# The second FFN product of a two-layer hybrid encoder, from slices of tokens to a 2x2x2 block scheme with seven products

## The chip, the cores and the metric

One core of a Trainium2 chip. TensorE (PE) multiplies a 128x128 block of weights by a tile of up to 512 columns and adds up in PSUM; VectorE (DVE), ScalarE (ACT) and GpSimd (POOL) work on tiles in SBUF (the first two on PSUM as well); SyncE (SP) issues most of the DMAs, GpSimd's queue a few. Each engine runs its own list of instructions in order, and the engines wait for each other by semaphores. The metric is the device time of one run in microseconds (us), lower is better. A profiled execution gives a trace; its span is the time from its first to its last instruction.

## What is computed

A two-layer encoder over 1024 prompt frames and 64 sample frames, 1088 tokens together: a state-space mixer, then attention, each followed by a gated feed-forward network (FFN). The change is in the FFN of both layers:

```python
D_MODEL = 1024; FFN_HIDDEN = 2816          # 22 tiles of 128
def rmsnorm(x, w):
    y = x * rsqrt(mean(x * x, axis=-1) + EPS)
    return y * w
def swiglu(u, w_in, w_out):
    g, up = split(u @ w_in, 2, axis=-1)
    return (silu(g) * up) @ w_out          # w_out: the second FFN product
# for each layer:
x = x + rmsnorm(mixer_or_attention(rmsnorm(x, nw[0])), nw[1])
x = x + rmsnorm(swiglu(rmsnorm(x, nw[2]), ffn_w_in, ffn_w_out), nw[3])
```

## The kernel before

Activations stand as columns: a tile has 128 features on the partitions and tokens along the free axis. Each float32 operand is split into a rounded high part and a low part, and each 128x128 block takes three matmuls: high weight by high input, high by low, low by high. So the work of a product is (row tiles) x (inner tiles) x 3 matmuls for each run of columns.

**The first FFN product** (1024 to 2 x 2816) already uses a 2x2x2 block scheme. The tokens are two blocks b of 512 and 576 columns (`BO`, `BN`), each of two quarters (`QS`: 256, 256, 288, 288 columns). `PRODS` lists seven products P1 to P7 of sums of blocks; `run_pair` computes them for one pair of hidden tiles (gate and value) for both b, adds them up while evicting from PSUM, and stores the hidden tile to DRAM. The first six hidden tiles of block 0 are computed plainly (`plain_pairs`). The sixteen pairs after them are done for both blocks, then six for block 1 alone.

**The second FFN product** (2816 to 1024) is plain. In `back`, the loop over `SL` takes three slices of 384, 384 and 320 tokens; for each slice it goes over eight row tiles m, and for each over three weight chunks of 8, 8 and 6 inner tiles (`KCH`). A task `loader` fetches the hidden tiles of a slice from DRAM into a staging tile `sg` and splits them into the `RX` and `R` tiles; the next slice is loaded while PE is at this one. When a slice is done, the task `end` normalizes it, adds the residual, writes it out, and in layer 0 also prepares the input of the next layer, all beside the next slice's matmuls.

**Weights.** The class `Weights` works through a list (`plan`) in order: `load` brings a chunk from DRAM into a raw tile (two of its own, and one or two lent from `RX`), `part` splits it into one of three `hl` tiles. The usual split is a ScalarE cast (the high part) and a VectorE subtraction (the low part). With `acc` set, ScalarE casts, ScalarE writes the negated high part to the low part's place, and a DMA on GpSimd's queue adds the weight to it from DRAM. Before, `acc` is set for a few chunks of the first FFN product and of the mixer only. A cast into an `hl` tile waits for the last matmul on the chunk that was there, three chunks earlier.

**What sets the order.** The matmuls' order is as the program is written (PE is scheduled by hand); `Stream` lets side tasks run ahead by a planned clock and the waits in their `yield`s (`EP_W`, `ER_W`, `EQ_W`). The other engines' order is made by a scheduler from priorities.

Of the kernel before, what the change touches and what calls it, by code (L numbers as in the profile page):

```python
# [8 lines left out]
F32 = mybir.dt.float32  # L9
# [39 lines left out]
ES = 0.5, 0.5, 0.0  # L49
OS = 1.9, 1.4  # L50
EP_W, ER_W, EQ_W = (9.4, 9.4, 2.2), (8.9, 8.9, 3.3), (11.0, 11.0)
# [4 lines left out]
LDP, ENP, ATP = 1500, (0, 0, 1500), 1000  # L56
# [3 lines left out]
RAWB, HLB, SGB = 2, 3, 5  # L60
# [6 lines left out]
NACC = 3  # L67

# [310 lines left out]
def hybrid_kernel(  # L379
# [42 lines left out]
    hd_ = [dr.tile([P, FT, T], F32, name=f"hscr{i}") for i in range(2)]  # L422
# [834 lines left out]

    def ffn_plan(layer):
        w1, w2 = w_f1[layer], w_f2[layer]
        W.plan(*[dict(src=[w1[i]], acc=t_ < NACC or t_ == NB0 - 1) for t_ in range(NB0) for i in (t_, FT + t_)])  # L1260
        for t_ in [*range(NB0, FT), *range(NB0)]:
            W.plan(dict(src=[w1[t_], w1[FT + t_]], pacc=t_ in (NB0, NB0 + 1)))
# [7 lines left out]
    def plain_pairs(ts, ops, hd, px, tmp):  # L1270

        n = ops.n
        first = ts == PGS[0]
        xs, ws = {}, {}
        for t_, i, q in [(t_, i, q) for t_ in ts for i, q in (((0, 0), (1, 0), (0, 1), (1, 1)) if first else ((0, 0), (0, 1), (1, 0), (1, 1)))]:
# [4 lines left out]
            if i == 0:  # L1280
                xs[t_, q] = tmp.tile([P, n], F32, tag=("p1", "u3")[q] + f"{t_ % 2}", name="x")
# [6 lines left out]
            def mult(ps):  # L1288
                with tc.high_priority(HIP):
                    V.tensor_tensor(x, ps[:, :n], x, op=ALU.mult)  # L1290
                nc.sync.dma_start(hd[:, t_, q * n:(q + 1) * n], x)
# [5 lines left out]
    def run_pair(t_, pr, bs, ends, ops, hd, px, tmp, apart=False):  # L1297
# [3 lines left out]
        for (p_, key, c0, i), b in [(x, b) for b in bs for x in PRODS] if apart else [(x, b) for x in PRODS for b in bs]:  # L1301
# [3 lines left out]
            def t_new(tag):  # L1305
                return tmp.tile([P, n], F32, tag=f"{tag}{b if len(bs) > 1 else t_ % 2}", name=tag)
# [15 lines left out]
            with tc.high_priority(HIP):  # L1322
# [16 lines left out]
                elif p_ == P4:  # L1339
# [3 lines left out]
                    nc.sync.dma_start(hd[:, t_, BO[b] + n:BO[b] + 2 * n], x["u3"])  # L1343
                else:
                    V.tensor_tensor(x["u2"], ps, x["u2"], op=ALU.add)
                    G.tensor_tensor(x["c22"], x["p1"], x["u2"], op=ALU.mult)
                    nc.sync.dma_start(hd[:, t_, BO[b]:BO[b] + n], x["c22"])
# [6 lines left out]
    def back(layer, start, cpost, xsrc, xmid, cpre, cpost2, xout, rb_out, done2):  # L1354

        hd = hd_[layer]
        dn, ops, phase, hid = [], [Ops(0, layer), Ops(1, layer)], [0], [{}, {}, {}]
        with ExitStack() as es:
# [3 lines left out]
            stage[0] = lambda: sgp.tile([P, 384], F32, tag="sg", bufs=SGB, name="sg")  # L1362

            def loader():

                for s, (o, n) in enumerate(SL):
                    yield 0, 0, lambda: phase[0] > (s > 0)
# [693 lines left out]
```

## Time and profile before

| | |
|---|---|
| time, median of three runs | 2938.9 us (2938.18 to 2941.24) |
| span of the profiled execution (no other time of it is given) | 2929.9 us |
| first FFN product, pairs for both blocks and for block 1, layer 0 | to 1315.6 us |
| second FFN product, layer 0 / layer 1, first matmul | 1315.6 / 2653.8 us |
| second FFN product, layer 1, last matmul | 2916.6 us |
| DMA traffic | 369 MB, mean 126 GB/s |

A row of the page's groups gives line, engine, operation, what is written and read, how often, and after the bar the total and mean time of one. Consecutive matmuls overlap, so the distance between two starts tells what one costs. A row of the stretches gives the stretch, then for PE, weight loads, DVE, ACT and POOL the busy time and in brackets the count, then the granted TensorE clock (1.00 is full speed), the share of the DMA engines' time, and GB/s. In a timeline a row has start, duration, engine, line, operation, and in square brackets how long the engine was idle before it and what ended that.

### The profile page before, as it was taken

How to read it: one execution, taken by the hardware profiler on the slowest of the kernel's cores; microseconds unless marked ns; L12 is line 12 of the kernel's file. 1: busy time of each engine (PE TensorE's matmuls, PEld its weight loads, DVE VectorE, ACT ScalarE, POOL GpSimd, SP SyncE). 2: the span in 40 equal slices, each digit the busy share in tenths (PEclk: the TensorE clock that was granted, in tenths of full speed). 3: DMA queues.
4: the chain of work that ended last, by engine and by line, in shares of the span. 5: the costliest groups of instructions: out<-in, count | busy, mean ns of one | idle time of the engine just before them, and what ended most of it. 6: DMA issues, size and time to landing. Idle time of an engine off the chain costs nothing.

```text
span 2929.9 us, 56271 instructions
## 1 busy us (share of the span) xinstructions
PE 2897.3 (99%) x21562; PEld 2858.7 (98%) x21562; DVE 2027.6 (69%) x4452; ACT 1403.6 (48%) x2535; POOL 718.9 (25%) x884
## 2 busy tenths in 40 slices
PE   8999999999999999999999999999999999999999
PEld 8999999999999999999999899999999999999998
DVE  7988878885867555583567887778688554575544
ACT  6655546454544222353445665556664222244443
POOL 1333333331022434350111000000131434351111
PEclk9999999999999999999999999999999999999999
DMA  4423333335564222345664322223476222245654
GB/s 138 133 92 106 104 98 109 100 117 165 165 187 137 76 81 77 108 151 163 207 192 154 98 74 72 65 69 108 132 204 179 83 77 81 75 154 178 225 171 135
DMA packets 203422, 369.12 MB, mean 126 GB/s; under 512 B 20752, under 2 KB 149488, under 8 KB 203152
## 3 DMA queue, kind: packets, MB, share of 16 engines
q1 hardware_dynamic: 199920, 354.97, 38.3%
q0 software_dynamic: 3232, 10.56, 2.0%
q8 instruction: 169, 2.77, 0.4%
q14 instruction: 101, 0.83, 0.1%
HBM read 298.24 MB, written 62.74 MB: 123 GB/s over the span
## 4 chain that ended last, share of the span: by engine, by line
PE 88%; DVE 6%; DMA 2%; ACT 2%; issue 1%; SPq 0%; POOL 0%; DVEq 0%; ACTq 0%; POOLq 0%
PE px L1314 9%; PE px L1315 9%; PE px L1313 9%; PE mm L467 8%; PE mm L469 8%; PE mm L468 8%; PE po L1515 6%; PE po L1516 6%; PE po L1514 6%; PE mmx L468 3%; PE mmx L469 3%; PE mmx L467 3%; PE ptp L1747 2%; PE po L1782 2%; PE S L1716 1%
## 5 line engine op out<-in xcount | busy, mean ns | idle before, releaser
L467 PE MATMUL mm<-r,hl 128*128 128x384 f32 (+2 forms) x1704 | 566.6, 333 | 2.6 <-DVE vt L1679 1.0
L469 PE MATMUL mm<-r,hl 128*128 128x384 f32 (+2 forms) x1704 | 549.6, 323 | 1.0 <-DVE hl L343 0.7
L468 PE MATMUL mm<-r,hl 128*128 128x384 f32 (+2 forms) x1704 | 549.3, 322 | 0.0
L343 DVE TENSOR_TENSOR hl<-raw,hl 128x1024 fp32r<-128x1024 f32 x216 | 256.3, 1187 | 216.6 <-ACT hl L342 208.9
L1314 PE MATMUL px<-r,hl 128*128 128x288 f32 (+1 forms) x1184 | 347.6, 294 | 0.0
L467 PEld LDWEIGHTS mm<-r,hl 128*128 128x128 f32 x1704 | 321.9, 189 | 4.9 <-DVE vt L1679 1.3
L469 PEld LDWEIGHTS mm<-r,hl 128*128 128x128 f32 x1704 | 321.1, 188 | 1.9 <-DVE hl L343 1.0
L468 PEld LDWEIGHTS mm<-r,hl 128*128 128x128 f32 x1704 | 322.2, 189 | 0.3
L1315 PE MATMUL px<-r,hl 128*128 128x288 f32 x1056 | 311.5, 295 | 0.0
L1313 PE MATMUL px<-r,hl 128*128 128x288 f32 x1056 | 310.4, 294 | 0.0
L342 ACT CAST hl<-raw 128x1024 fp32r<-128x1024 f32 x216 | 216.8, 1004 | 162.5 <-PE po L1516 101.6
L493 POOL TENSOR_TENSOR ssum<-ssum,sq 128x256 f32<-128x256 f32 (+3 forms) x97 | 125.5, 1295 | 616.9 <-ACT sq L492 601.3
L1314 PEld LDWEIGHTS px<-r,hl 128*128 128x128 f32 x1184 | 222.4, 188 | 0.0
L1315 PE MATMUL px<-rx,hl 128*128 128x256 f32 x768 | 214.2, 279 | 3.6 <-DVE hl L343 3.5
L1313 PE MATMUL px<-rx,hl 128*128 128x256 f32 x768 | 213.9, 278 | 0.4 <-DVE x L1290 0.4
L1515 PE MATMUL po<-rx,hl 128*128 128x384 f32 (+1 forms) x624 | 202.0, 324 | 0.2
L1313 PEld LDWEIGHTS px<-r,hl 128*128 128x128 f32 x1056 | 198.9, 188 | 0.1
L1315 PEld LDWEIGHTS px<-r,hl 128*128 128x128 f32 x1056 | 198.9, 188 | 0.0
L1514 PE MATMUL po<-rx,hl 128*128 128x384 f32 (+1 forms) x608 | 197.7, 325 | 0.0
L1516 PE MATMUL po<-rx,hl 128*128 128x384 f32 (+1 forms) x608 | 196.7, 324 | 0.0
L1314 PE MATMUL px<-rx,hl 128*128 128x256 f32 x640 | 178.4, 279 | 0.0
L1514 PE MATMUL po<-r,hl 128*128 128x384 f32 (+1 forms) x448 | 148.4, 331 | 0.0
(367 smaller groups left out, 7890.1 us busy)
## 6 DMA issues: line engine op xcount, KB each, us to landing
raw<-in_w_f_dram SPq DMA_DIRECT2D x154, 512.0 KB, 3.7
rx<-in_w_f_dram SPq DMA_DIRECT2D x54, 512.0 KB, 3.7
raw<-in_w_in_dram SPq DMA_DIRECT2D x40, 512.0 KB, 3.7
MT<-ascr SPq DMA_DIRECT2D x48, 384.0 KB, 4.3
sg<-hscr SPq DMA_DIRECT2D x88, 192.0 KB, 3.4
raw<-in_w_f_dram SPq DMA_DIRECT2D x44, 384.0 KB, 3.2
raw<-in_w_so_dram SPq DMA_DIRECT2D x32, 512.0 KB, 3.7
raw<-in_w_o_dram SPq DMA_DIRECT2D x19, 512.0 KB, 3.6
```

What stands on the lines that cost most here:

```text
L342: self.nc.scalar.copy(h, v)
L343: (eng or self.eng or self.nc.vector).tensor_tensor(lo, v, h, op=ALU.subtract)
L467: PE.matmul(ps[:, :n], h_, xh, start=(first and i == 0), stop=False)
L468: PE.matmul(ps[:, :n], h_, xl, start=False, stop=False)
L469: PE.matmul(ps[:, :n], l_, xh, start=False, stop=(last and i == nk - 1))
L493: (eng or G).tensor_tensor(ssum[:, :n], ssum[:, :n], q[:, :n], op=ALU.add)
L1313: PE.matmul(ps, wh, ah[:, k, :], start=(k == 0), stop=False)
L1314: PE.matmul(ps, wh, al[:, k, :], start=False, stop=False)
L1315: PE.matmul(ps, wl, ah[:, k, :], start=False, stop=(k == 3))
L1514: PE.matmul(ps[:, :n], wh, xh, start=(k == 0), stop=False)
L1515: PE.matmul(ps[:, :n], wh, xl, start=False, stop=False)
L1516: PE.matmul(ps[:, :n], wl, xh, start=False, stop=(k == FT - 1))
```

## The change

The second FFN product becomes a 2x2x2 block scheme as well: output rows in two halves of four tiles, inner tiles in two halves of eleven (`KH`), and each b's tokens in two quarters. The seven products are the outermost loop (`SEQ`): P1, P6, P2 and P5 for both b, then P3, P7, P4 for b 0, then the same for b 1, whose weights are fetched and split again. A weight chunk is now six or five inner tiles (768 or 640 columns), and where both b share it, it is held until the second has used it.
- The sums of hidden tiles that the products need are made in SBUF by `hidden`, on VectorE, when a tile is finished, and all seven operands go to DRAM (`hc`). The hidden tiles are computed in another order (`T_PLAIN`, `T_BOTH`, `T_TAIL`), so that the two tiles of a sum are neighbours.
- The sums of weights are made by a side task `w2_sums` beside the first product: four loads, four VectorE operations and four stores for each of sixteen pieces a layer. P1, P2 and P3 read `w_f2` itself and have `acc` set; P4 to P7 read the sums.
- `evict` adds each product to its output blocks (one copy, seven additions on VectorE); the output is held by quarters, and `end` runs by quarter, four times a layer.
- `loader` reads several hidden tiles with one DMA, straight into the low part's tile, without a staging tile.
- In layer 1, `evv` waits until the norms of its slice are there.

```diff
-KCH = ((0, 8), (8, 8), (16, 6))
+    W2S = {P6: 0, P7: 1, P5: 2, P4: 3}
+    SEQ = ((P1, (0, 1)), (P6, (0, 1)), (P2, (0, 1)), (P5, (0, 1)), (P3, (0,)), (P7, (0,)), (P4, (0,)), (P3, (1,)), (P7, (1,)), (P4, (1,)))
+    KCH = (0, 6), (6, 5)
...
-        for s in range(NSL):
-            for m in range(KD):
+        for p_, _ in SEQ:
+            for j in range(4):
                 for k0, nk in KCH:
-                    W.plan(dict(src=[w2[m][:, k0 * P:(k0 + nk) * P]], n=nk * P))
+                    W.plan(dict(src=[w2_of(layer, p_, j)[:, k0 * P:(k0 + nk) * P]], n=nk * P, acc=p_ in (P1, P2, P3)))
...
+    def w2_sums(layer, yet):
+        w2, wd = w_f2[layer], wd_[layer]
+        for j in range(4):
+            for c in range(0, KH * P, SUM_C):
...
+                for t_, m, a in ((b22, j + 4, KH * P + c), (b12, j + 4, c), (b11, j, c), (b21, j, KH * P + c)):
+                    nc.sync.dma_start(t_, w2[m][:, a:a + SUM_C])
+                V.tensor_tensor(b22, b22, b12, op=ALU.subtract)
+                V.tensor_tensor(b12, b12, b11, op=ALU.subtract)
+                V.tensor_tensor(b11, b22, b11, op=ALU.add)
+                V.tensor_tensor(b21, b21, b11, op=ALU.subtract)
+                for i, t_ in enumerate((b11, b22, b12, b21)):
+                    nc.sync.dma_start(wd[:, i, j, c:c + SUM_C], t_)
+                yield 0, SUM_GAP
...
+            def hidden(t_, b, x, z, late=None):
+                if not kh:
+                    s3 = stage[0]()[:, :n] if late is None else late[:, k * n:(k + 1) * n]
+                    out(OPI["a11"], x)
+                    out(OPI["s3"], total(s3, x, z, ALU.subtract))
...
+                out(OPI["a12"], x)
+                out(OPI["a22"], z)
+                out(OPI["s1"], total(z0, z0, z, ALU.add))
+                s2 = total(stage[0]()[:, :n], z, s3, ALU.subtract)
+                out(OPI["s2"], s2)
+                out(OPI["s4"], total(stage[0]()[:, :n], x, s2, ALU.subtract))
...
+            for x, (p_, bs) in enumerate(SEQ):
+                if x == len(SEQ) - 1:
+                    W.lent.cap = 0
+                    st.spawn(end_load(3))
+                for j in range(4):
+                    ws = []
+                    for b in bs:
+                        n = ops[b].n
+                        ps = px.tile([P, 512], F32, tag="mm", name="po")
+                        for c, (k0, nk) in enumerate(KCH):
+                            if b == bs[0]:
+                                ws.append(W.get())
+                            h, v = ws[c]["w"]
+                            for k in range(k0, k0 + nk):
...
+                                PE.matmul(ps[:, :n], wh, xh, start=(k == 0), stop=False)
+                                PE.matmul(ps[:, :n], wh, xl, start=False, stop=False)
+                                PE.matmul(ps[:, :n], wl, xh, start=False, stop=(k == KH - 1))
+                            if b == bs[-1]:
+                                W.put()
+                        evict(p_, b, j, ps[:, :n])
```

Two places of the built programs show what this does to the order. The first is TensorE at the start of a weight chunk in the second FFN product of layer 0 (`po` is the PSUM tile, `rx` the input, `hl` the weights; the number is that of the buffer's use). Before:

```order
L1514 MATMUL po_16083<-rx_15063,hl_16021 128x384 [waits Activation_49]
L1515 MATMUL po_16083<-rx_15063,hl_16021 128x384
L1516 MATMUL po_16083<-rx_15063,hl_16021 128x384 [waits DVE_49]
L1514 MATMUL po_16083<-rx_15068,hl_16021 128x384
L1515 MATMUL po_16083<-rx_15068,hl_16021 128x384
```

TensorE at the start of the second weight chunk of product P2, layer 0, after the change:

```order
L1675 MATMUL po_17085<-rx_16517,hl_16966 128x256
L1676 MATMUL po_17085<-rx_16518,hl_16966 128x256
L1677 MATMUL po_17085<-rx_16517,hl_16966 128x256
L1675 MATMUL po_17085<-rx_16635,hl_16966 128x256
L1676 MATMUL po_17085<-rx_16636,hl_16966 128x256
L1677 MATMUL po_17085<-rx_16635,hl_16966 128x256
L1675 MATMUL po_17085<-rx_16635,hl_17047 128x256 [waits Activation_49]
L1676 MATMUL po_17085<-rx_16636,hl_17047 128x256
L1677 MATMUL po_17085<-rx_16635,hl_17047 128x256 [waits DMASW7_49]
L1675 MATMUL po_17085<-rx_16635,hl_17047 128x256
```

The third matmul of a chunk, the first with the low part of the weight, waited for VectorE and now waits for a DMA of GpSimd's queue (`DMASW`). The second place is ScalarE beside these matmuls. Before:

```order
L342 CAST hl_16050<-raw_15857 128x1024 [waits DVE_49,PE_49,Activation_49]
L1376 CAST r_15972<-sg_15978 128x384 [waits DMAHW0_49]
L1376 CAST r_15977<-sg_15982 128x384 [waits DMAHW1_49]
L1376 CAST r_15986<-sg_15987 128x384 [waits DMAHW2_49]
L1529 COPY y_15939<-po_15940 128x384 [waits DMASW0_49,DMAHW4_49,PE_49,Pool_49]
L342 CAST hl_16073<-rx_15877 128x768 [waits DMAHW3_49,DVE_49,Activation_49]
```

ScalarE in product P2 of layer 0 after the change (`ssum` belongs to the norms):

```order
L343 CAST hl_17078<-rx_16949 128x768 [waits DMAHW1_49,DVE_49,PE_49]
L1446 CAST r_17003<-r_17004 128x1024 [waits DMAHW7_49]
L344 ACTIVATE hl_17078<-hl_17078 128x768 [waits Activation_49]
L1446 CAST r_17017<-r_17018 128x768 [waits DMAHW1_49]
L497 ACTIVATE ssum_17120<-rx_16351 128x256 [waits DVE_49]
L343 CAST hl_17141<-raw_16970 128x640 [waits DMAHW5_49,DMASW6_49,PE_49]
L344 ACTIVATE hl_17141<-hl_17141 128x640 [waits Activation_49]
```

ScalarE has a second operation for each such chunk, and the cast into `hl_17141` waits for TensorE's last use of `hl_16966`, which had the buffer before, and for the DMA that wrote there.

More of the change, by code (lines that the diff above doesn't have):

```diff
@@ L1398, in end @@
-                steps = rb_steps(ss, n, out, ER_W[s], more=more)
+                if more is None:
+                    yield 0, EP_W[q]
+                steps = rb_steps(ss, n, out, ER_W[q], more=more)
                 if more is not None:
```

342 lines of the change are left out of this document (216 added, 126 removed).

## The prediction

> **What bounds the kernel now.** The page comes first: its span and its engines, then the stretches of time around the second FFN product of each layer (both layers, cut at its first and last matmul), then who makes TensorE wait.
>
> ```profile
> span 2929.9 us, 56271 instructions
> PE 2897.3 (99%) x21562; PEld 2858.7 (98%) x21562; DVE 2027.6 (69%) x4452; ACT 1403.6 (48%) x2535; POOL 718.9 (25%) x884
> PE 88%; DVE 6%; DMA 2%; ACT 2%; issue 1%; SPq 0%; POOL 0%; DVEq 0%; ACTq 0%; POOLq 0%
> ```
>
> TensorE (PE) is busy for 99% of the span and is 88% of the chain of waits. The stretches (microseconds, then busy time and count of PE, weight loads, VectorE, ScalarE, GpSimd, then granted clock, DMA share, GB/s) show the same of the two stages that the change touches:
>
> ```profile
> 1020.00:1316.00 296.00, 296.00 (x2355) 296.00 (x2354) 176.54 (x301) 105.06 (x176) 123.47 (x105) 1.00 0.33 104
> 1480.00:1556.00 76.00, 75.79 (x497) 75.14 (x496) 55.33 (x95) 40.20 (x63) 13.99 (x9) 1.00 0.66 211
> 2737.00:2840.00 103.00, 103.00 (x598) 102.94 (x597) 51.78 (x75) 42.41 (x68) 12.03 (x10) 1.00 0.67 216
> PE px L1315 <- DVE hl L343: 3.5, 2, 1.8
> ```
>
> In the first product (1020 to 1316) and in the second (the other two rows) PE never stops; the largest group of PE waits in the whole span is 3.5 us. So columns taken away from PE are time saved, as long as nothing new makes PE wait. That second half of the sentence decides here.
>
> **What the change removes.** A matmul is priced by the distance between starts, not by its listed duration, since matmuls overlap. First and last start of unbroken runs, by the columns that they stream:
>
> ```profile
> 1419.67 0.34 PE L1514 MATMUL po<-r,hl 128*128 128x384 f32 x1
> 1425.96 0.34 PE L1514 MATMUL po<-rx,hl 128*128 128x384 f32 x1
> 1549.76 0.31 PE L1514 MATMUL po<-rx,hl 128*128 128x320 f32 x1
> 1558.85 0.31 PE L1516 MATMUL po<-rx,hl 128*128 128x320 f32 x1
> 1299.73 0.29 PE L1313 MATMUL px<-r,hl 128*128 128x288 f32 x1
> 1307.13 0.30 PE L1315 MATMUL px<-r,hl 128*128 128x288 f32 x1
> 863.76 0.28 PE L468 MATMUL mmx<-rx,hl 128*128 128x256 f32 x1
> 870.00 0.28 PE L469 MATMUL mmx<-rx,hx 128*128 128x256 f32 x1
> 1019.72 0.28 PE L1313 MATMUL px<-rx,hl 128*128 128x256 f32 x1
> 1021.02 0.28 PE L1315 MATMUL px<-rx,hl 128*128 128x256 f32 x1
> ```
>
> 384 columns: 36 intervals in 6.29 us, 0.1747 each. 320: 62 in 9.09, 0.1466. 288: 56 in 7.40, 0.1321. 256: 55 in 6.24 (0.1135) in one stage, 11 in 1.30 (0.118) in another; I take 0.116. Before, a layer has 8 x 22 x 3 = 528 matmuls for each of the slices of 384, 384 and 320: 1056 x 0.1747 + 528 x 0.1466 = 261.9 us. After, 7 products x 4 row tiles x 11 x 3 = 924 at 256 and 924 at 288: 924 x (0.116 + 0.1321) = 229.2 us. **Saved: 32.7 us a layer** (30.6 to 35.0 with 0.118 and 0.1135), if PE stays fed.
>
> **What it adds to the weights, the term that decides.** For P1, P2 and P3 the low part of a weight chunk is no longer one VectorE subtraction: ScalarE casts, ScalarE negates, and GpSimd's queue adds the weight from DRAM with an accumulating DMA. The third matmul of the chunk waits for it. Before has a few such chains in other stages; this is one, from cast to matmul:
>
> ```profile
> 58.57 1.05 ACT L336 CAST hl<-raw 128x1024 fp32r<-128x1024 f32 x1 [1.61 <-PE mmp L469]
> 60.09 1.04 ACT L337 ACTIVATE hl<-hl 128x1024 fp32r<-128x1024 f32 x1
> 61.44 0.90 POOL L338 DMA_DIRECT2D hl<-in_w_in_dram  x1 [1.92 <-ACT hl L337]
> 66.66 0.45 PE L469 MATMUL mm<-r,hl 128*128 128x384 f32 x1 [0.27 <-DMA hl<-in_w_in_dram]
> ...
> DMA to landing us min/median/max: 4.1/7.7/10.8
> ...
> hl<-in_w_f_dram POOLq DMA_DIRECT2D x2, 512.0 KB, 7.5
> half<-in_w_f_dram POOLq DMA_DIRECT2D x2, 256.0 KB, 5.4
> ...
> hl<-in_w_f_dram POOLq DMA_DIRECT2D x3, 512.0 KB, 10.3
> ...
> 826.00:850.00 24.00, 24.00 (x189) 24.00 (x188) 6.78 (x12) 14.16 (x20) 11.28 (x14) 1.00 0.81 219
> 2215.00:2262.00 47.00, 44.44 (x387) 43.85 (x386) 38.70 (x66) 20.93 (x29) 8.50 (x8) 1.00 0.66 179
> L342 ACT CAST hl<-raw 128x768 fp32r<-128x768 f32 x22 | 18.4, 837 | 0.0
> ```
>
> 8.1 us passed from the cast to the matmul. The 23 accumulating DMAs of the span landed 4.1 to 10.8 us after issue. The chunks here are 768 and 640 columns, 384 and 320 KB, which no such DMA has; the rows at 7.5 and 5.4 are from 2215 to 2262, where the DMA share is 0.66 as in the second product, and give 6.4 and 5.9 us between them. A cast of 768 is 0.84 us, of 640 by the same rate 0.73; the handover from ScalarE to the DMA was 0.31 (61.13 to 61.44). Chain: 0.84 + 0.84 + 0.31 + 6.4 = **8.4 us** for the six-k chunk, 0.73 + 0.73 + 0.31 + 5.9 = **7.7 us** for the five-k chunk. (That PE may start two matmuls early, 0.23, I set against the unseen step from PE to ScalarE.)
>
> How much time is there? There are three `hl` buffers, so a chunk's cast waits for the last matmul of the chunk three before it. Before, a chunk is needed two whole chunks after that, 42 to 48 matmuls at 0.1747, 7.3 to 8.4 us. Now, where both halves b share a chunk, the five-k chunk's buffer comes free only when the six-k chunk of the row tile before has been used by the second half, and it is needed after 15 matmuls at 0.1321 and 18 at 0.116: 4.07 us. Row by row:
> - P2: four row tiles, each late by 7.7 - 4.07 = 3.6 us: 14.5.
> - P1: its first buffer is freed after three of the last pair's seven products, 4 x 12 x 0.1321 = 6.3 us ahead: late by 2.1; then three row tiles at 3.6: 13.0.
> - P3, one half at a time: three buffers, each held for the chain (mean 8.05) and the use (33 x 0.116 / 2 = 1.91): a chunk every 3.32 us in place of 1.91, eight chunks: 11.3. For the other half 3.41 in place of 2.18: 9.8.
>
> **Waits added: 48.6 us a layer.** With both landings at 4.1 the same steps give 22.7; with the 10.3 us that three of 512 KB had between 826 and 870 (DMA share 0.81 in its first part), scaled to 8.8 and 8.1, they give 78.7. I stay in the middle, as the two DMA shares of 0.66 agree. P4 to P7 keep cast and subtraction, 0.84 + 0.96 at 768 columns, which fits into 3.8 us and more.
>
> **Smaller terms.** In the last product only two raw weight tiles are left, and a chunk holds one for a load (3.2 us, row below), a cast and a subtraction: 5.0 / 2 = 2.5 us against 2.18, eight chunks: 2.6 us a layer (0 to 8, since with more traffic loads land later).
>
> ```profile
> raw<-in_w_f_dram SPq DMA_DIRECT2D x154, 512.0 KB, 3.7
> ...
> raw<-in_w_f_dram SPq DMA_DIRECT2D x44, 384.0 KB, 3.2
> ...
> L1431 DVE TENSOR_TENSOR y<-y,r 128x384 f32<-128x384 f32 x16 | 8.2, 544 | 0.0
> ...
> 53.31 2.19 PE L706 MATMUL dtn<-stk,dtT 64*128 64x32 f32 x18
> ...
> 56.00:58.00 2.00, 2.00 (x9) 2.00 (x9) 0.46 (x1) 0.44 (x1) 0.00 (x0) 0.50 0.00 0
> 58.00:60.00 2.00, 2.00 (x11) 2.00 (x10) 1.35 (x5) 1.43 (x2) 0.45 (x2) 0.64 0.00 0
> ```
>
> The weight sums (64 a layer, 352 columns, some 0.5 us by the L1431 row) and the operand sums (88, some 0.45) put 70 us on VectorE in the first product, some 400 us long, where it is 60% busy: 78%, hidden beside PE. What could show is SP's in-order queue: each sum's stores wait for VectorE, its next loads wait for those stores, and the raw weights of the next pair stand behind them; a pair lasts 21 us, its load 3.7, so I take 1 us a layer (0 to 8). The moved evictions and the operand loads, four to a DMA, are hidden beside PE likewise. Norms by quarter: at the end of layer 0 the third quarter has the two last products, 2 x 4 x 33 x 0.1321 = 35 us, for 38 us of planned waits, and slice 0's keys, values and queries run first: 1 us in all (0 to 6).
>
> PE that starts and stops may lose clock: from 56 to 58 the granted clock was 0.50, soon after 2.2 us of tiny matmuls, and in the 4 us from there 20 matmuls of 320 columns ran where 27 fit: 1.1 us lost. Of the seven long waits a layer I let some two or three pay that: 3 us (0 to 8). On this the Trainium skill, "TensorE: Matmul & The Clock Gate", section "Part 1: The HAM clock gate", says that the clock halves only after an idle window of about 3.4 us. By that rule waits of 3.6 us would almost never fill a window and the 3 us would be nothing; the 0.50 row came without any idle time, so the row speaks for more than the rule.
>
> **Sum.** -32.7 + 48.6 + 2.6 + 1 + 3 = +22.5 us a layer, +45 for two, +1 at the layer's end: the span goes from 2929.9 to 2976. The page gives the profiled execution a span only; the three timed runs, median 2938.9, lie 9.0 us above it, which I add back: **2985 us**.
>
> **Rivals.**
> - *The accumulating DMA lands like a plain load* (3.2 us for 384 KB): chains of 5.2 and 4.9 us, waits of 0.8 a row tile, 10.7 us a layer; with 2.6 and 1 the change is 18.4 us faster a layer: 2902, **faster**. For it: the chunks are smaller than 512 KB. Against it: the quickest of 23 took 4.1, at 256 KB. Chance 0.10. The Trainium skill gives this case a rule: "DMA: Bandwidth & Descriptors", section "Anatomy of one DMA — SWDGE (gpsimd) path", fits a DMA from GpSimd's queue by 2.0 us plus bytes over 436 GB/s. By it the two would take 2.75 and 2.9 us and the time would be some 2893 (an estimate by that page); the 7.5 us row at 512 KB, 3.2 by the fit, does not agree.
> - *It lands at its quickest, 4.1*: waits of 22.7, -6.4 a layer with the same two terms: 2926, still **faster**. The point from which the change loses is waits of some 29 us a layer, landings near 4.6. Chance 0.12.
> - *Traffic makes it land late*: the second product now moves 28.8 MB of weights, 11.5 MB again for the accumulation and 21.4 MB of operands a layer, where it moved 34.6 and 12.3. With 78.7 of waits: 3045, **slower**. For it: the DMA share is 0.67 already. Against it: PE's waits stretch the stage. Chance 0.18.
> - That the weights do not go this way is out: the rows of the built order show the DMA and the wait.
>
> **Chances and range.** The forecast (waits of 33 to 62 a layer, 2950 to 3020) has 0.55, within 0.2% (what a measurement of this kernel can tell from no change) 0.05. Slower is 0.55 + 0.18 = 0.73, faster 0.10 + 0.12 = 0.22. The range runs from 2920, all landings at 4.1 and no other term, to 3065, the late landings with some of the upper ends; it leaves out the plain-load case and the tail of the late one.
>
> **What would show it.** Right: in the second product PE waits for the DMA on `hl` in P1, P2 and P3 and in no other product, about 3.6 us once a row tile in P1 and P2 and 1.4 a chunk in P3; the accumulating DMAs land in 6 us; P5, P6 and P7 run without a gap. Wrong: landings under 4.6, waits on raw loads in P4 and P7 instead, or VectorE waits on PE in the first product.

## The result and the profile after

The changed kernel takes **3218.9 us** (3213.3 to 3222.3), the kernel before 2938.5 beside it: ratio 1.0953, 95% interval 1.0937 to 1.0968. The direction was forecast; the time is 154 us above the top of the range.

The page of after, its head and one row of its DMA issues:

```profile
span 3216.9 us, 58502 instructions
PE 2940.1 (91%) x22096; PEld 2875.4 (89%) x22096; DVE 2201.9 (68%) x4821; ACT 1450.6 (45%) x2587; POOL 762.4 (24%) x967
...
hl<-in_w_f_dram POOLq DMA_DIRECT2D x32, 384.0 KB, 7.3
```

TensorE went from 99% busy to 91%: 277 us of the span are now time in which it stands. Its busy time rose as well, by 43 us, although it has 7/8 of the columns to stream in the second product: a sign that it ran at a lower clock.

What TensorE waits for in after (us in total, times, longest):

```profile
PE po L1677 <- DMA hl<-in_w_f_dram: 108.2, 37, 6.8
PE px L1353 <- DVE u L1368: 37.9, 19, 3.9
PE nst L508 <- DVE ssum L1543: 30.0, 2, 15.9
PE px L1355 <- DVE hl L350: 17.8, 7, 3.7
PE px L1353 <- DVE p L1370: 10.9, 7, 2.1
```

Row one is the forecast wait for the accumulating DMA (`po` is the second product). Rows two, four and five stand in the first product (`px`), where the forecast had 1 us a layer in all, and row three at the norms of layer 0's end. The four FFN stages, from first to last matmul, first and second product of layer 0, then of layer 1 (busy time and count of PE, weight loads, VectorE, ScalarE, GpSimd; granted clock, DMA share, GB/s); before, then after:

```profile
913.00:1315.60 402.60, 400.38 (x3195) 400.01 (x3194) 239.16 (x403) 140.11 (x230) 162.52 (x138) 1.00 0.31 97
1315.60:1580.30 264.70, 264.49 (x1609) 263.77 (x1608) 144.81 (x219) 121.23 (x197) 37.06 (x28) 1.00 0.59 185
2250.50:2653.80 403.30, 400.74 (x3194) 400.05 (x3193) 246.63 (x408) 143.69 (x234) 161.49 (x138) 1.00 0.31 97
2653.80:2916.40 262.60, 262.60 (x1597) 262.46 (x1596) 121.88 (x165) 103.70 (x159) 31.81 (x24) 1.00 0.57 181
```

```profile
919.90:1380.60 460.70, 418.57 (x3195) 411.48 (x3194) 318.49 (x523) 137.77 (x220) 162.05 (x141) 0.97 0.46 145
1380.60:1712.80 332.20, 261.10 (x1867) 256.04 (x1866) 145.55 (x252) 146.14 (x231) 57.07 (x68) 0.89 0.73 199
2421.20:2885.50 464.30, 421.62 (x3194) 414.39 (x3193) 321.16 (x524) 138.25 (x218) 160.68 (x140) 0.97 0.46 144
2885.50:3203.70 318.20, 256.73 (x1863) 251.58 (x1862) 132.91 (x203) 131.76 (x188) 57.92 (x62) 0.91 0.73 203
```

The first products, whose matmuls are unchanged in number, take 58 and 61 us longer; the second ones 67.5 and 55.6. The rest of the 287 us of span lies between: the stretch from layer 0's last product to the first attention score went from 37.0 to 63.7, the attention stage grew by 11.5, the stage ahead of the first FFN by 6.9.

Below, each run is compared by its time and by these stages, cut in the same way in its own trace.

### The profile page after: what moved, and what is told of

It reads as the page before. It is cut to its first block, busy times and chain, and to the rows that moved or that the text cites. A ratio compares the mean times of both kernels' runs of the same rounds, so it can differ in the third digit from the quotient of the medians.

```text
span 3216.9 us, 58502 instructions
## 1 busy us (share of the span) xinstructions
PE 2940.1 (91%) x22096; PEld 2875.4 (89%) x22096; DVE 2201.9 (68%) x4821; ACT 1450.6 (45%) x2587; POOL 762.4 (24%) x967
## 5 line engine op out<-in xcount | busy, mean ns | idle before, releaser
L1354 PE MATMUL px<-r,hl 128*128 128x288 f32 (+1 forms) x1184 | 354.7, 300 | 0.0
L1353 PE MATMUL px<-r,hl 128*128 128x288 f32 x1056 | 319.1, 302 | 37.4 <-DVE u L1368 12.7
L1355 PE MATMUL px<-r,hl 128*128 128x288 f32 x1056 | 317.2, 300 | 4.7 <-DVE hl L350 4.7
L350 DVE TENSOR_TENSOR hl<-raw,hl 128x1024 fp32r<-128x1024 f32 (+2 forms) x188 | 211.0, 1124 | 121.2 <-ACT hl L349 118.9
L1353 PE MATMUL px<-rx,hl 128*128 128x256 f32 x768 | 219.8, 286 | 27.4 <-DVE u L1368 25.2
L1677 PE MATMUL po<-r,hl 128*128 128x288 f32 (+1 forms) x728 | 216.9, 298 | 29.5 <-DMA hl<-in_w_f_dram 26.8
L1353 PEld LDWEIGHTS px<-r,hl 128*128 128x128 f32 x1056 | 204.1, 193 | 43.5 <-DVE u L1368 14.6
L1677 PE MATMUL po<-rx,hl 128*128 128x256 f32 (+1 forms) x504 | 161.6, 321 | 83.7 <-DMA hl<-in_w_f_dram 81.5
L349 ACT CAST hl<-raw 128x1024 fp32r<-128x1024 f32 (+2 forms) x188 | 178.4, 950 | 126.7 <-PE po L1677 71.2
L1355 PE MATMUL px<-rx,hl 128*128 128x256 f32 x768 | 217.6, 283 | 13.2 <-DVE hl L350 13.2
L1354 PEld LDWEIGHTS px<-r,hl 128*128 128x128 f32 x1184 | 229.5, 194 | 0.0
L1675 PE MATMUL po<-r,hl 128*128 128x288 f32 (+1 forms) x728 | 216.2, 297 | 0.5 <-ACT hl L349 0.5
L1676 PE MATMUL po<-r,hl 128*128 128x288 f32 (+1 forms) x728 | 215.6, 296 | 0.0
L501 POOL TENSOR_TENSOR ssum<-ssum,sq 128x256 f32<-128x256 f32 (+1 forms) x111 | 120.5, 1086 | 380.7 <-ACT sq L500 365.7
L1355 PEld LDWEIGHTS px<-r,hl 128*128 128x128 f32 x1056 | 204.2, 193 | 5.1 <-DVE hl L350 5.1
L1677 PEld LDWEIGHTS po<-rx,hl 128*128 128x128 f32 x504 | 109.0, 216 | 90.9 <-DMA hl<-in_w_f_dram 87.9
```

The lines of the kernel that those rows point to most:

```text
L349: self.nc.scalar.copy(h, v)
L350: (eng or self.eng or self.nc.vector).tensor_tensor(lo, v, h, op=ALU.subtract)
L501: (eng or G).tensor_tensor(ssum[:, :n], ssum[:, :n], q[:, :n], op=ALU.add)
L1353: PE.matmul(ps, wh, ah[:, k, :], start=(k == 0), stop=False)
L1354: PE.matmul(ps, wh, al[:, k, :], start=False, stop=False)
L1355: PE.matmul(ps, wl, ah[:, k, :], start=False, stop=(k == 3))
```

## The experiments

### The two weight edits, apart and together

e1_no_acc lets P1, P2 and P3 take the cast and VectorE's subtraction again:

```diff
-    W.plan(dict(src=[...], n=nk * P, acc=p_ in (P1, P2, P3)))
+    W.plan(dict(src=[...], n=nk * P))
```

e2_no_wsums leaves the weight sums out (P4 to P7 then read blocks of `w_f2` itself, so its times count and not its output; the same holds for e4 and all that stands on it), e3_wsums_dma keeps their loads and stores and leaves out the arithmetic, e4_neither is e1 and e2 together:

```diff
-        if p_ in W2S:
-            return wd_[layer][:, W2S[p_], j, :]
-        m, kh = {P1: (j, 0), P2: (j, 1), P3: (j + 4, 1)}[p_]
+        m, kh = {P1: (j, 0), P2: (j, 1), P3: (j + 4, 1), P6: (j + 4, 0), P7: (j, 0), P5: (j, 1), P4: (j + 4, 1)}[p_]
...
-                st.spawn(w2_sums(layer, yet), 12.0)
+                yet.append(layer)
```

> The changed kernel, but P1, P2 and P3 split their weight chunks with a cast and a VectorE subtraction like P4 to P7, without the accumulating DMA. Theory (the accumulating DMA's waits, 108 us in the profile, and the clock lost beside them): 3219 falls by 110 to 130, to about 3095, and PE's waits for the DMA on hl are gone. Rival (VectorE is the limit of the second product, and the DMA only stood in for it): PE waits for VectorE's subtraction there instead, at least 50 of the 108 us come back, 3150 or more.

> The changed kernel without the weight sums: the side task that loads, sums and stores them is left out, and P4 to P7 take blocks of w_f2 itself, so the result is not the FFN's. Theory (the sums make VectorE, and behind it PE, stand still in the first product, above all in its first 200 us): the first product falls from 461 to about 425 us a layer and the time to about 3140. Rival (the operand sums and the additional stores of hidden do it): under 25 us in all, about 3200.

> The changed kernel with the loads and stores of the weight sums but without their VectorE operations, so that plain pieces of w_f2 are stored in place of the sums. Theory (VectorE reaches a weight sum before its load has landed, and what stands behind it in order waits): nearly all that leaving the sums out gains is gained here too, about 3150. Rival (SP's queue and the DMA traffic of 46 MB a layer do it, raw weights come late): about 3205.

> The changed kernel with neither the accumulating DMA in the second product nor the weight sums (P4 to P7 take blocks of w_f2 itself, so the result is not the FFN's). If the two are separate costs, the gains add: 3219 - 125 - 80, about 3015. If one hides behind the other, it comes out at least 30 above that. What is left over 2939 - 65 (the columns saved) would be the operand sums, the end of layer 0 and the clock: some 140 us.

Measured: e1 3067.3 (1.0431, 1.0400 to 1.0461), e2 3128.1 (1.0637, 1.0606 to 1.0668), e3 3200.3 (1.0882, 1.0832 to 1.0933), e4 2974.4 (1.0114, 1.0085 to 1.0144). So the accumulating DMAs cost 151.5 us and the weight sums 90.8; together 242, and e4 is 244.5 below after: the two add up. About 36 us over before are left. Against their theories, e1 gained more than the 110 to 130 us, e2 came out as forecast (3140, first products 425), and e4 is 41 us below the 3015 forecast for it.

Of the 151.5 us of the accumulation, 144 lie in the second products, and the first products give another 3 to 4 a layer. In e1 the second products take:

```profile
1377.30:1637.80 260.50, 237.97 (x1868) 235.71 (x1866) 170.20 (x281) 122.81 (x201) 32.45 (x38) 0.96 0.66 207
2807.40:3053.10 245.70, 235.94 (x1863) 233.16 (x1862) 158.39 (x234) 109.57 (x159) 31.43 (x32) 0.99 0.67 213
```

332.2 to 260.5 and 318.2 to 245.7, 72 us a layer. Of this, 54 is the wait (108.2 for both layers) and 22 is busy time: 261.1 against 238.0, 256.7 against 235.9, for the same matmuls, with the granted clock at 0.89 and 0.91 in after and at 0.96 and 0.99 in e1. (The waits on the split weights are 3 to 4 us a layer longer than in after and take that much back.) Where the clock goes is seen in stretches of 1 us around two waits of P1 in after, one of 3.43 us that ends at 1400.6 and one of 2.26 us that ends at 1414.0:

```profile
1398.00:1399.00 1.00, 0.00 (x0) 0.00 (x0) 0.44 (x2) 0.75 (x1) 0.86 (x1) 1.00 0.90 181
1400.00:1401.00 1.00, 0.38 (x1) 0.38 (x2) 0.14 (x1) 0.00 (x0) 0.00 (x0) 0.50 1.01 371
1405.00:1406.00 1.00, 1.00 (x6) 1.00 (x6) 0.74 (x1) 0.23 (x1) 0.00 (x0) 0.50 0.12 34
1407.00:1408.00 1.00, 1.00 (x10) 1.00 (x9) 0.00 (x0) 0.53 (x1) 0.00 (x0) 1.00 0.03 8
1412.00:1413.00 1.00, 0.00 (x0) 0.00 (x0) 0.00 (x0) 0.28 (x1) 0.43 (x1) 1.00 1.01 179
1415.00:1416.00 1.00, 1.00 (x11) 1.00 (x10) 0.00 (x0) 0.12 (x1) 0.00 (x0) 1.00 0.98 196
```

After the first wait 6 matmuls start in a microsecond instead of 10 or 11, for some 7 us; after the second one nothing is lost.

The length of a single wait does not decide this. All 42 stretches at 0.50 in after start a whole multiple of 3.413 us apart, and each lasts 3.41 us or a multiple of it (the one that the end of the trace cuts off is 3.32): the clock changes only at the lines of a fixed grid. Counted over this grid from 60 us on, every one of the 39 windows at full clock in which TensorE was busy for 0.44 of the time or less was followed by 0.50, and none of the 818 windows with 0.46 or more was. The wait of 2.26 us fell across a line and left the first of its two windows busy for 0.54; one of only 1.78 us (it ends at 3198.1) stood with other idle time in a window busy for 0.41, and the clock fell. In the other runs the border is less sharp: in e1 and e12 windows between 0.43 and 0.57 went either way.

The weight sums cost 37.7 and 39.2 us in the first products (after 460.6 and 464.4, e2 422.9 and 425.2; without the accumulation it is much the same, e1 457.5 and 460.6, e4 419.0 and 422.8), and 4.1 and 10.4 in the stages ahead of them. e3 splits that: with loads and stores alone the first products take 441.0 and 445.4, so by these stages about half of it is the DMAs and half the arithmetic with its waits. By its total e3 speaks for the DMAs, as expected by the rival: it is 72 us above e2, of the 91. The difference lies in the stages ahead, which are 20.0 and 13.4 us longer than in e2: with no sums to wait for, 57 of the 128 weight-sum DMAs of layer 0 are issued ahead of the first FFN product, against 21 in after, so part of their cost has only moved. The DMAs are the larger part by the total and half by the first products, and neither theory holds whole. (The 46 MB in the expectation are those of both layers; a layer has 23.)

### How the weight sums cost: waits, bytes or place

e7_sums_spaced, on e1, puts planned time between loads and sums. e12_more_stores, on e4, adds stores that wait for nothing of their own. e9_sums_ahead, on e1, makes the sums one stage earlier and on GpSimd.

```diff
# e7
                     nc.sync.dma_start(t_, w2[m][:, a:a + SUM_C])
+                yield 0, SUM_GAP / 2
...
-                yield 0, SUM_GAP
+                yield 0, SUM_GAP / 2
# e12, in hidden
+                for e in range(4):
+                    nc.sync.dma_start(ex_[layer][:, 4 * b + e, t_, :n], x)
# e9: spawned in the state-space stage and in the attention stage, 26 us apart
-                V.tensor_tensor(b22, b22, b12, op=ALU.subtract)
+                G.tensor_tensor(b22, b22, b12, op=ALU.subtract)
...
+        st.spawn(w2_sums(0, yet), 12.0)
...
+        st.spawn(w2_sums(1, yet), 12.0)
```

> The kernel without accumulating DMAs (3067.3 us; all of the computation is made), with 9 us of planned time between the loads of the weight sums and the sums and stores, instead of 18 us behind each group; bytes and instructions are the same. Theory (a store that waits at the head of SP's queue for its sums holds back the raw weights of the first product): the first products go from 457 and 461 to 420 to 440 us, 3010 to 3040 in all. Rival (the traffic of 128 loads and stores of 180 KB a layer is what delays the raw weights, in whatever order): 450 to 465 us, 3050 to 3075.

> The kernel without accumulating DMAs and without weight sums (2974.4 us; its output is not the FFN's), with 176 further stores a layer (128 or 144 KB, 24 MB) of a hidden tile that is stored there already, put in SP's queue right behind that store, so that none of them has anything of its own to wait for. The weight sums brought 128 loads and stores and 23 MB, and 38 us to each first product. Theory (it is what their entries wait for at the head of SP's queue, not their bytes): the first products stay within 419 to 428 us, 2974 to 2990 us in all. Rival (the bytes or the number of entries delay the raw weights): 440 to 460 us each, 3015 to 3055 us in all.

> The kernel without accumulating DMAs (3067.3 us, all of the computation is made), with the weight sums of layer 0 made during the stage before its FFN and those of layer 1 during the attention stage, on GpSimd, and not in the first products; the same loads, sums and stores. Theory (it is the place: in the first products they stand in SP's queue ahead of raw weights that are wanted at once): the first products fall from 457 and 461 to 419 to 425 us, the stages that take the sums in grow by less than 10 us each, 2980 to 3005 in all. Rival (23 MB a layer and 128 entries in SP's queue cost as much anywhere): the stages ahead grow by 25 to 40 us each, 3050 to 3080 in all.

**e7**: 3071.5 (1.0451, 1.0433 to 1.0468), first products 459.3 and 459.2. This decides nothing: SP's order came out almost as it was, since the planned time steers TensorE's order, and loads that depend on nothing were put early again.

**e12**: 2987.9 (1.0167, 1.0152 to 1.0182), first products 426.2 and 428.1, 7 and 5 us over e4's. 24 MB and 176 entries a layer more in the same queue cost a fraction of the 38 us. What VectorE waited for in layer 0's first product until the last six tiles, e12 (915.5 to 1235), then after (919.9 to 1240):

```profile
DVE tt L315 <- POOL tt L297: 35.2, 16, 4.6
DVE hl L350 <- ACT hl L349: 27.3, 36, 1.1
DVE sg L1414 <- POOL c L1384: 20.0, 14, 2.0
```

```profile
DVE tt L315 <- POOL tt L297: 24.1, 13, 7.1
DVE sg L1412 <- POOL c L1385: 22.0, 19, 1.9
DVE wsum L1298 <- DMA wsum<-in_w_f_dram: 13.9, 4, 5.2
DVE hl L350 <- ACT hl L349: 12.8, 18, 1.1
DVE wsum L1299 <- DMA wsum<-in_w_f_dram: 11.4, 5, 4.0
```

In e12 the raw weights come late too (VectorE waits 35 us in all for GpSimd's sums of them), and TensorE loses little: single waits stay under 5 us. In after, VectorE stands up to 7.1 us for the same, and another 25.3 us, up to 5.2 at a time, at the weight sums themselves, for loads that have not landed. The evictions of the first product stand behind it in VectorE's list, and TensorE runs out of PSUM tiles: its waits for `u` and `p` above. At the head of SP's queue, loads of the sums stood 23.8 us in that stretch until earlier stores had landed, and their stores 10.1 us for VectorE. So for the larger part it is what the entries wait for, on VectorE and at the head of SP's queue, and not their bytes. Two things limit this reading: e12 added stores only, so loads without waits were not tried, and time at the head of SP's queue is not in itself lost (in e4 it stands 103.0 us at stores of one of GpSimd's tiles, and TensorE hardly waits).

**e9**: 3043.0 (1.0355, 1.0339 to 1.0370). The first products fell to 420.6 and 425.7, as without the sums; but the stage ahead of layer 0's FFN grew by 34.9 us over e1's, the attention stage by 10.5. The attention stage just missed the theory's limit of 10 us, the other stage went as the rival has it, and the total lies between the two. It is the fastest kernel here that makes the whole computation, and slower than before.

### What is left: the end of the first product

In layer 0's first product of e4 TensorE stands 14.1 us, 10.3 of them in the last 85 us, where the last six tiles run for one half of the columns; in layer 1's it is 16.0, 9.1 of them there. `p1`, `u2`, `u3` and `c22` are small SBUF tiles in which the products of a pair of hidden tiles are added up. e6_sums_gpsimd makes the operand sums on GpSimd; e8_p1_two gives `p1` two buffers; e10_both is both; e13_tail_two takes all four small tiles from two sets in turn; e15_tail_gpsimd is e13 with e6. All stand on e4.

```diff
# e6, e10, e15, in hidden
-                    V.tensor_tensor(t, x_, y_, op=op)
+                    G.tensor_tensor(t, x_, y_, op=op)
# e8, e10
-    bufs=2 if tag == "u3" or (tag == "p1" and not b) else 1
+    bufs=2 if tag in ("u3", "p1") else 1
# e13, e15
-                return tmp.tile([P, n], F32, tag=f"{tag}{b}", ...)
+                c = b if len(bs) > 1 else t_ % 2
+                return tmp.tile([P, 288], F32, tag=f"{tag}{c}", ...)[:, :n]
```

> The kernel without accumulating DMAs and without weight sums (2974.4 us, its output not the FFN's), with the operand sums of the hidden tiles made on GpSimd instead of VectorE. In 2974.4 the first FFN products take 419 and 423 us against 403 before the change. Theory (VectorE stands at an operand sum, whose input GpSimd has yet to make, with evictions queued behind it): 403 to 408 us each, 2940 to 2950 us in all. Rival A (the three added stores of each hidden tile are the cost): 417 to 425 us, 2970 to 2978. Rival B (GpSimd is then late with the sums of the first product's weights): over 425 us each, over 2980.

> The kernel without accumulating DMAs and without weight sums (2974.4 us; its output is not the FFN's, since the products with summed weights read unsummed blocks), with two buffers instead of one for the tile p1 of the second half of the columns. In 2974.4 the waits of TensorE in the first FFN products stand in their last 85 us, where ScalarE waits 28.7 us in 6 pieces for GpSimd's product c22 (it reads p1, the only buffer of it) before it can evict the next P1. Theory (the single buffer makes one pair of tiles wait for the pair before it): the first products go from 419 and 423 us to 405 to 410, 2945 to 2955 us in all. Rival (VectorE's splits for the second product, which begin in the same stretch, are what is late): 416 to 423 us, 2968 to 2978 us.

> The kernel without accumulating DMAs and without weight sums (2974.4 us; its output is not the FFN's), with the operand sums on GpSimd and two buffers for the tile p1 of the second half of the columns together. Apart, neither brought the first products below 419 us: with GpSimd's sums ScalarE still waited 28.7 us at the end for the single p1, with two p1 VectorE still waited 9.6 us for GpSimd's product at its operand sums. Theory (two covers of one delay at the end of the first products; only both together free TensorE): 405 to 412 us each, 2950 to 2960 us in all. Rival (it is the loads and splits of the second product's operands, which begin there in pieces of 512 KB): 417 to 424 us each, 2970 to 2995 us in all.

> The kernel without accumulating DMAs and without weight sums (2974.4 us; its output is not the FFN's), with the tiles p1, u2, u3 and c22 of the last six tiles of the first product, where one half of the columns is left, taken from both halves' buffers in turn, as they were before the change. With two buffers for p1 alone VectorE still waited 9.6 us, and with GpSimd's sums besides it waited 19.1 us (7 pieces) at u2 for the product c22 that reads the only u2. Theory (p1 and u2, each with one buffer, tie a tile to GpSimd's product of the tile before it): the first products go from 419 and 423 us to 405 to 411, 2945 to 2960 us in all. Rival (the 512 KB loads of the second product's operands, for which ScalarE waits up to 5 us in that stretch): 417 to 424 us, 2968 to 2980 us in all.

> The kernel without accumulating DMAs and without weight sums (2974.4 us; its output is not the FFN's), with the last six tiles' p1, u2, u3 and c22 in two sets of buffers and the operand sums on GpSimd together. With two sets alone VectorE waited 9.6 us in that stretch for GpSimd's product at its operand sums; with GpSimd's sums and two p1 it waited 19.1 us for the single u2. Theory (both together leave VectorE nothing to wait for there but the splits of the next operands): the first products go from 419 and 423 us to 408 to 414, 2955 to 2975 us in all, as GpSimd's sums cost 3 us in each second product. Rival (the stretch is set by the operand loads and the clock): 417 to 425 us, 2980 to 2997 us in all.

| run | us | ratio (95%) | first product, layer 0 / 1 | second product, layer 0 / 1 |
|---|---|---|---|---|
| e4 | 2974.4 | 1.0114 (1.0085 to 1.0144) | 419.0 / 422.8 | 260.0 / 247.7 |
| e6 | 2994.3 | 1.0191 (1.0176 to 1.0206) | 422.5 / 425.4 | 264.3 / 250.8 |
| e8 | 2974.9 | 1.0121 (1.0104 to 1.0138) | 420.2 / 423.9 | 260.9 / 247.2 |
| e10 | 2992.6 | 1.0180 (1.0163 to 1.0197) | 421.8 / 420.8 | 266.9 / 255.1 |
| e13 | 2978.1 | 1.0143 (1.0121 to 1.0165) | 418.3 / 424.5 | 260.4 / 249.1 |
| e15 | 2994.7 | 1.0193 (1.0178 to 1.0208) | 419.6 / 418.8 | 273.2 / 261.5 |

No theory held. By the stages e6 is as its rival A has it, by its time as rival B; the other four are as their rival has it. Every edit took away the wait that it aimed at, and the next one stood behind it. With those waits gone, e15's VectorE (its timeline, with the idle time ahead of an instruction and what ended it) shows the last:

```profile
1307.10 0.44 DVE L1377 TENSOR_TENSOR u<-px,u 128x288 f32<-128x288 f32 x1
1314.10 1.06 DVE L1446 TENSOR_TENSOR rx<-rx 128x864 fp32r<-128x864 f32 x1 [6.55 <-ACT rx L1445]
1315.07 0.45 DVE L1379 TENSOR_TENSOR u<-px,u 128x288 f32<-128x288 f32 x1
...
1338.07 1.36 DVE L1446 TENSOR_TENSOR r<-r 128x1152 fp32r<-128x1152 f32 x1 [6.93 <-ACT r L1445]
```

VectorE stands 6.6 and 6.9 us at the split of the second product's operands, since ScalarE stands at the copy ahead of it until their load lands, and evictions (`u<-px`) come behind. (The second split starts 3.4 us past the end of this first product, at 1334.7.) That speaks for the operand loads, but no run took them out of that stretch: for these 16 to 20 us a layer (in layer 0 the waits rose from 2.2 to 14.1 us and the busy time from 400.4 to 404.9) the cause stays argued.

### What is left: the end of layer 0

e5_late_norms lets TensorE have other work ahead of the second norm's transposes, e11_end_gpsimd takes work from VectorE, e14_order finishes the first half of the columns earlier, e16_order_late is e14 with e5. All stand on e4.

```diff
# e5, e16
-EQ_W = (11.0, 11.0, 11.0, 11.0)
+EQ_W = (26.0, 30.0, 30.0, 11.0)
# e11, in end: the residual addition and the three additions of squares
-    V.tensor_tensor(y[h], y[h], xs[h], op=ALU.add)
+    G.tensor_tensor(y[h], y[h], xs[h], op=ALU.add)
...
# e14, e16: SEQ
-    (P1, (0, 1)), (P6, (0, 1)), (P2, (0, 1)), (P5, (0, 1)), (P3, (0,)), (P7, (0,)), (P4, (0,)), (P3, (1,)), (P7, (1,)), (P4, (1,))
+    (P1, (0, 1)), (P6, (0, 1)), (P2, (0,)), (P5, (0,)), (P3, (0,)), (P7, (0,)), (P4, (0,)), (P2, (1,)), (P5, (1,)), (P3, (1,)), (P7, (1,)), (P4, (1,))
```

> The kernel without accumulating DMAs and without weight sums (2974.4 us; its output is not the FFN's, since the products with summed weights read unsummed blocks), with the planned wait ahead of the second norm's transposes raised from 11 us to 26, 30 and 30 for the first three quarters, so that TensorE has other products ahead of them in its order. In 2974.4 TensorE stands 15.5 us inside layer 0's second product and 15.9 us behind it at these transposes. Theory (the transposes stand too early in TensorE's order): both stalls go for the larger part, layer 0's second product 260 to about 245 us, the stretch to the first attention score 63 to about 50, 2945 to 2955 us in all. Rival (VectorE's backlog of splits and sums is itself what the next stage needs): the stalls turn up at the next stage's projections, 2970 to 2980 us.

> The kernel without accumulating DMAs and without weight sums (2974.4 us; its output is not the FFN's), with the residual additions and the sums of squares of the layer's end on GpSimd instead of VectorE. Some 5.6 us of each quarter leave VectorE (two additions of 1.2 to 1.8, two of 1.2 to 1.35, 0.7 and 0.4), whose backlog of quarters 0 to 2 the norms wait for. Theory (VectorE has more than it can do in the last 60 us, since by the products' order no quarter is whole before the last three products): the stretch to the first attention score falls from 63 to 45 to 55 us, layer 0's second product from 260 by up to 5, 2955 to 2968 us in all. Rival (the chain of one quarter, not VectorE's load, sets it, and GpSimd is slower): 63 us or more, 2972 to 2990 us in all.

> The kernel without accumulating DMAs and without weight sums (2974.4 us; its output is not the FFN's), with the second product's order changed so that the first half of the columns is finished 5 products (some 80 us) before the end instead of 3 (some 48 us); two products then load and split their weights twice (16 more half blocks, 5.6 MB). Theory (the work on four quarters of the output crowds into the last products and what follows, which is the cost of products outermost): the stretch to the first attention score falls from 63 to 40 to 50 us and the 15 us stall inside layer 0's second product goes, for 5 to 10 us of more splits in each layer; 2945 to 2962 us in all. Rival (the last quarter's own chain is what TensorE waits for, whenever the others end): 60 to 64 us to the first score, 2975 to 2995 us in all.

> The kernel without accumulating DMAs and without weight sums, with the first half of the columns finished 5 products before the end (2987.2 us alone; its output is not the FFN's), and with the planned wait ahead of the second norm's transposes raised from 11 to 26, 30 and 30 us as well. Theory (TensorE stands 14.4 and 12.6 us at transposes that stand ahead of other work in its order; with the quarters done earlier the next stage has work that can go first): layer 0's second product 262 to 247 us, the stretch to the first score 60 to 45 to 52, 2960 to 2970 us in all. Rival (the next stage's first products need the same quarters): the stall moves behind the second product, 68 to 76 us to the first score, 2980 to 2992 us in all.

| run | us | ratio (95%) | second product, layer 0 | to the first score |
|---|---|---|---|---|
| e4 | 2974.4 | 1.0114 (1.0085 to 1.0144) | 260.0 | 63.4 |
| e5 | 2979.1 | 1.0140 (1.0125 to 1.0156) | 245.5 | 74.8 |
| e11 | 3004.3 | 1.0229 (1.0213 to 1.0244) | 267.5 | 70.6 |
| e14 | 2987.2 | 1.0167 (1.0150 to 1.0184) | 261.6 | 59.8 |
| e16 | 2992.5 | 1.0178 (1.0160 to 1.0196) | 246.5 | 77.4 |

The rival each time (e11 is even above its rival's time, and e16 just above): the sum of the two stretches stays at 320 to 338 us. TensorE's waits at the layer's end (1500 to 1640 in e4, 1500 to 1680 in e16):

```profile
PE nst L508 <- DVE ssum L1541: 31.4, 2, 15.9
PE nst L508 <- POOL ssum L501: 4.0, 1, 4.0
```

```profile
PE nst L508 <- DVE ssum L1541: 20.8, 2, 18.2
PE mm L476 <- DVE r L1466: 4.8, 2, 2.6
PE mm L477 <- DVE hl L363: 2.7, 1, 2.7
```

Moved behind other work, the stall of 15 us inside the product is gone, and the next stage's first products wait (`mm`, for `r` and `hl`), then its norms, for the same quarters. How full VectorE is in the last 48 us of e4's second product, and how little of that time TensorE gets, is one row:

```profile
1543.00:1591.10 48.10, 32.62 (x232) 32.17 (x232) 46.44 (x107) 26.62 (x64) 8.48 (x13) 0.82 0.63 192
```

Before, a slice was whole after each third of the product; now the second quarter is whole only ahead of the last three products and the third and fourth within them, and VectorE, 46.4 of 48.1 us busy, has their scalings, sums and splits to do at once. That this load is the cause stays argued: e11 took work off VectorE, and the stretch grew to 70.6 us. A product order that spreads them further than e14 was not tried.

## Why the prediction was right in direction and wrong in size

By its own steps, for both layers, on the profiled executions (287 us between the spans):

| step | forecast | measured |
|---|---|---|
| columns saved | -65 | -53 (busy 262.6 to 235.9 in layer 1 of e1, where the starts are 0.114 and 0.132 us apart in the median, as forecast) |
| waits for the accumulating DMA | +97 | +108 |
| lost clock in the second products | +6 | +44 (after against e1) |
| last product's raw tiles; waits on split weights | +5 | +10 |
| sums and loads beside the first product | +2 | +119, and 18 in the stages ahead |
| layer 0's end | +1 | +41 (14.1 in the product, 26.7 behind it) |

- **The wait for the DMA was right.** It stands in P1, P2 and P3 and in no other product, and the landings were 7.3 us for 384 KB against 6.4 and 6.4 for 320 KB against 5.9. In layer 0 the four row tiles of P1 waited 4.1, 3.4, 2.3 and 2.4 us (12.2, forecast 13.0), P2 16.8 (14.5), P3 10.9 and 12.7 (11.3 and 9.8). In P3 it came in three to seven waits of up to 6.8 us and not as 1.4 us a chunk. (The forecast counts 23 accumulating DMAs in the kernel before; its trace has 22.)
- **The direction did not hang on it.** Without its 48.6 us of waits and 3 us of clock the forecast's own sum comes to some 2880 us, faster than before; e1, without the accumulation, took 3067.3. What makes it slower even so are the terms that the forecast put at next to nothing, below.
- **The clock was mis-sized, 3 us a layer against 22.** The step "of the seven long waits a layer I let some two or three pay" failed. All 16 DMA waits of 3.29 us and more in the two second products were followed by a stretch at 0.50. The Trainium skill, "TensorE: Matmul & The Clock Gate", section "Part 1: The HAM clock gate", says that activity is judged in free-running windows of about 3.4 us and that the clock of a core running alone is either full or half. The trace agrees: its grid is 3.413 us, and the granted clock is 0.50 or 1.00. The forecast argued from that page that waits of 3.6 us would almost never fill a window. Here a window did not have to be filled with idle time: 0.44 of it busy was still too little, and a wait of 2.35 us was enough (1597.6, followed by 0.50 until 1601). So that reading was too strict, and the row from 56 to 58, which stood against it, should have weighed more.
- **"Hidden beside PE" failed for the first product, the largest miss.** The step compared VectorE's busy share, 60% plus the sums, with 100%. VectorE did have the time (318.5 of 460.7 us busy), but it works in order, and the sums brought it instructions that wait for DMAs and for GpSimd. The price named, SP's queue, was put at 1 us a layer; e3, which has the queue without VectorE's sums, still takes 18.1 and 20.1 us more than e2 in the first products. The stores without waits of e12 show that bytes and entries of stores were a small part, 7 and 5 us. 77 of the 119 us are the weight sums; some 6 went with the accumulation (e1); 36 stay in e4, where nearly two thirds of the waits stand at the end of the stage, and were not won back by any run.
- **Layer 0's end failed as well, +41 us against +1.** The step set 38 us of planned waits against 35 us of products. The measured chain is longer; VectorE, which then has three quarters to do at once, is 46.4 of 48.1 us busy in e4, but no run shows that this is the cause.
- **The last product's raw tiles** were not the place: of the 10 us of waits on split weights only 2.0 stand in the last product, in layer 1, and the rest in P7 and P4 for b 0. P6 and P5 ran without a gap, as the forecast's signs had it, P7 did not.
- **The rival of late landings** (3045) came nearest in time but not by its mechanism: landings were 7.3 us against its 8.8, waits 54 us a layer against 78.7. It too took the landing as the only thing that could grow.

## What to carry to other kernels

A wait costs its own length and, where waits leave TensorE busy for less than some 0.45 of a 3.4 us window, half of the next window besides: here 54 us of waits a layer came with 22 us of lost clock. Several short waits in one window count together. Work put on an engine with idle time is hidden only if its instructions find their inputs ready; ask what stands behind each new instruction that waits for a DMA, not how busy the engine is. And a loop order that makes all outputs whole in the last products moves the work on them from beside the matmuls to behind them.

## What the hardware did that was not expected

- The granted clock fell to 0.50 for 3.41 us or a multiple of it after waits of 3.29 us and more each time, after waits of 1.78 to 3.09 us sometimes (1.78, 2.35 and 3.09 us: yes; 2.26, 2.79 and 3.02 us: no). What told the two apart in after was the busy share of a window on a fixed grid of 3.413 us: 0.44 and less against 0.46 and more.
- 176 more stores of 128 and 144 KB a layer, 24 MB, lengthened the first products by 7 and 5 us only.
